# Sums of a block product chained in PSUM, the splits of a left factor spread over the next pair, and another order of the first loads of W_out

## The chip, the cores and the metric

The kernel runs on one core of a Trainium2 chip. What counts is the device time of one execution in microseconds (us). It was run three times: 2336.66, 2331.77 and 2335.1 us, median 2335.1 us. Engines are named as in the profile: PE is TensorE (its matmuls; PEld is its loading of weights), DVE is VectorE, ACT is ScalarE, POOL is GpSimd, SP is SyncE, which issues the loads. POOL issues the stores.

## The reference

One layer of an encoder trunk on x of 1024 tokens by 1024 features, float32: a half-step feed-forward network, a token mixing, and a second half-step feed-forward network, each between two norms.

```python
def _swiglu(x, w_in, w_out):                       # w_in 1024 x 5632, w_out 2816 x 1024
    g, u = jnp.split(x @ w_in, 2, axis=-1)
    return (jax.nn.silu(g) * u) @ w_out

h = _swiglu(_rms_norm(x, ffn1_pre_norm), ffn1_w_in, ffn1_w_out)
x = x + 0.5 * _rms_norm(h, ffn1_post_norm)
m = _token_mixing(_rms_norm(x, mix_pre_norm), w_mix_in, ..., w_mix_out, pos)
x = x + _rms_norm(m, mix_post_norm)
h = _swiglu(_rms_norm(x, ffn2_pre_norm), ffn2_w_in, ffn2_w_out)
x = x + 0.5 * _rms_norm(h, ffn2_post_norm)
```

`_token_mixing` projects its input once (`u @ w_in`, 6656 columns) into queries, keys, values and gates of a retention (its queries and keys get a rotary embedding) and of a neighbourhood attention, computes both, gates and projects them. The change touches the two feed-forward networks and that projection.

## The kernel before, in words

**Numbers in two parts.** A float32 product is made from three matmuls: each operand is split into a high part (a copy into the matmul format by ACT, L61) and a low part (the rest, a subtraction on DVE, L62). `mm3` (L86) multiplies high by high, high by low and low by high into one PSUM bank of 128 x 512. A product of a 128 x 512 weight block with a 512 x 512 quarter of x is four such groups, 12 matmuls.

**Seven products in place of eight.** x (transposed, 1024 x 1024) is held as the seven left operands of Winograd's form of Strassen's scheme: a11, a12, a22 and the sums s1 to s4 (class `Winograd`). A *pair* (`Pairs.run`, L364) takes two weight columns blocks, g (b11, b21) and u (b12, b22), forms four combinations t1 to t4 of them on DVE, multiplies seven times, and combines the seven banks into four results c11, c12, c21, c22. The lines of the combinations: ACT copies the bank of a11 into c11 (L377); DVE adds s2's bank to that for c12 (L382), a12's for c11 (L385), s3's bank to c12 for c21 (L390), s1's to c21 for c22 (L393) and to c12 (L394), a22's to c21 (L398), s4's to c12 (L401). `out(j)` gives the tile of result j, `done(j)` is called when it is complete. The products run in the order a11, s2, a12, s3, s1, a22, s4; each has its own bank, of six. `behind` only fixes an order on DVE. PE, DVE and ACT work through their own instructions in the order in which the scheduler has put them, and wait for each other by semaphores.

**Led pairs.** While x is still being normed and transposed, `lead` and `leads` already make the products a11 and a12 of the first pairs. The first three stay in their banks ("held"); further ones ("saved": three in FFN 1, one in FFN 2, none in the mixing projection) are copied to SBUF. These pairs have five products left when their turn comes.

**Input projection** (`ffn_in`, L405): 22 pairs, each of a gate and an up column. `done` applies silu to the gate results on ACT (L415) and multiplies by the up results on DVE (L417); the two multiplies are called up0 and up1 in the prediction, after the halves of the tile `gt` that they fill. Then `put` is called.

**Left factors of the output projection** (`LeftFactors`, L422): G = silu(g) * u becomes the left operand of the second matrix product, again in Winograd's form. Two successive pairs give a group of four blocks. When the second is there, POOL forms the four sums s1 to s4 (L441), and for each of the seven factors ACT makes a high part in a buffer `gth` (L447; four of them), DVE a low part in place (L448), and POOL stores both to DRAM (L68), 256 KB each. All seven are called one after the other at the end of the group's second pair, in the order a11, s1, s3, a22, s2, a12, s4. There are eleven groups in each network.

**Output projection** (`ffn_out`, L513): seven products of eleven steps each; step n needs one block of G (`Blocks`, L453, a load of 0.5 MB on SP) and one 128 x 512 block of W_out or of a combination of it. W_out lies in four quadrants, `tiles[i][j]`, each in three loads of 1, 1 and 0.75 MB. `LOADS` (L33) names the steps at which the twelve loads are issued: the first quadrant's at 0, 2 and 4, after the blocks of G of steps 0 and 1, 3, 5. The first four steps take their blocks of the first quadrant from loads of their own (L618). POOL forms the combinations t1 to t4 in `prepare` (L633) from steps 8, 19, 24 and 30 on. G's buffers and most tiles of W_out lie where the input projection had its operands, so their loads wait for its last matmuls. SP issues in order.

**The mixing projection** (L1163 to L1201): twelve pairs, four plain, then rotary and silu pairs in turn, and two sigmoid pairs. `done` rotates a rotary pair's results, two halves on POOL and two on DVE (`rotate`, L868 to L871), or applies the function on ACT, and stores the result. The results lie in buffers `ev`, six.

## Time and profile before

| | |
|---|---|
| runs | 2336.66, 2331.77, 2335.1 us |
| profiled execution | 2335.32 us, of which 2333.2 us are the span from the first to the last instruction |
| mean granted clock of PE | 0.989 |
| moved by DMA | 442.03 MB, mean 189 GB/s |

The stages by the trace: norm and leading products of FFN 1 up to 69 us, its input projection to 468 us, its output projection to about 700 us, the mixing to about 1673 us (the pairs of its projection from 749 to 1034 us), the leading products of FFN 2 to 1700 us, its input projection to 2104 us, its output projection to the end.

How to read the lines of the profile: a row of a timeline has the start in us from the span's start, the duration in us, engine, line of the kernel, operation, tile written <- tiles read, and, in square brackets, how long the engine was idle before and what ended that. Rows of the chain that ended last have start, duration, what. A row of a table of stretches has the stretch, its length, busy time (and instructions) of PE, PEld, DVE, ACT, POOL, then the granted clock of PE (1.00 is full), the mean busy share of the DMA engines and GB/s. In a group's row "wl<-wraw,wh" is the tile written and those read.

### The profile page before, as it was taken

Reading aid. Unit: us, or ns where it says so; the run is one execution under the profiler, and the core shown is the slowest. Engines: PE = TensorE matmul, PEld = TensorE weight load, DVE = VectorE, ACT = ScalarE, POOL = GpSimd, SP = SyncE. Lnnn points to the kernel's source line nnn. Section 1 sums busy time; section 2 is a strip of 40 time slices with the busy share of each in tenths; the row PEclk is TensorE's granted clock in tenths of the full one; section 3 lists DMA queues with packets and bytes.
Section 4 is the critical chain, followed back from the end, with each engine's and each line's share of the span. In section 5 each row is a group of like instructions: output and inputs, shape, how many; then the busy total and the mean of one; then the engine's idle time right before and its main releaser. Section 6 shows DMA issues by size and latency. Waiting matters only on the chain.

```text
span 2333.2 us, 30479 instructions
## 1 busy us (share of the span) xinstructions
PE 2230.0 (96%) x10288; PEld 1839.0 (79%) x10288; DVE 1677.9 (72%) x2833; ACT 1010.2 (43%) x2102; POOL 806.1 (35%) x889
## 2 busy tenths in 40 slices
PE   6999999989997999999999999999799999999997
PEld 5778888868886887777888888787578888887886
DVE  7888887844459768969875687546988888884443
ACT  6433443422335222248885675315544433443232
POOL 5333424259424134411001222101443333426942
PEclk9999999999999999999999999999999999999999
DMA  4445444498545442257654466766534534449764
GB/s 144 148 141 176 143 156 148 168 388 296 204 162 188 169 167 100 89 186 243 214 170 169 163 220 227 264 222 206 168 127 149 185 140 173 140 149 369 296 245 167
DMA packets 148220, 442.03 MB, mean 189 GB/s; under 512 B 18465, under 2 KB 46241, under 8 KB 145953
## 3 DMA queue, kind: packets, MB, share of 16 engines
q1 hardware_dynamic: 109344, 312.13, 39.6%
q0 software_dynamic: 38720, 127.96, 14.7%
q8 instruction: 82, 1.34, 0.2%
q14 instruction: 74, 0.60, 0.1%
HBM read 303.70 MB, written 140.51 MB: 190 GB/s over the span
## 4 chain that ended last, share of the span: by engine, by line
PE 59%; issue 13%; DVE 12%; POOL 6%; DMA 6%; ACT 3%; POOLq 0%; SPq 0%; DVEq 0%; ACTq 0%
PE ps L90 18%; PE ps L88 18%; PE ps L89 18%; DVE wl L62 3%; POOL cmb L441 2%; DMA g1s<-gth 1%; DMA g<-g0a 1%; PE pt L89 1%; PE pt L90 1%; PE pt L88 1%; DMA wraw<-in_dram 1%; ACT wh L61 1%; POOL rstd L98 1%; DVE tmp L118 1%; DVE t L379 1%
## 5 line engine op out<-in xcount | busy, mean ns | idle before, releaser
L62 DVE TENSOR_TENSOR wl<-wraw,wh 128x512 fp32r<-128x512 f32 x516 | 382.9, 761 | 80.4 <-ACT wh L61 79.2
L61 ACT CAST wh<-wraw 128x512 fp32r<-128x512 f32 x524 | 306.0, 618 | 247.7 <-DVE wraw L396 67.9
L62 DVE TENSOR_TENSOR wl<-x,wh 128x512 fp32r<-128x512 f32 x146 | 137.8, 956 | 192.1 <-ACT wh L61 191.0
L88 PE MATMUL ps<-wh,g 128*128 128x512 f32 x484 | 191.5, 397 | 11.3 <-DMA g<-g0a 6.4
L89 PE MATMUL ps<-wl,g 128*128 128x512 f32 x484 | 191.1, 395 | 0.0
L90 PE MATMUL ps<-wh,g 128*128 128x512 f32 x484 | 190.4, 393 | 0.0
L61 ACT CAST wh<-x 128x512 fp32r<-128x512 f32 x146 | 88.6, 620 | 216.4 <-PE pt L90 93.0
L441 POOL TENSOR_TENSOR cmb<-gt 128x512 f32<-128x512 f32 x44 | 63.7, 1464 | 320.6 <-DVE gt L417 320.6
L543 POOL TENSOR_TENSOR x<-x 128x512 f32<-128x512 f32 x110 | 158.8, 1469 | 34.2 <-DMA x<-in_dram 24.2
L415 ACT ACTIVATE c<-c 128x512 f32<-128x512 f32 x88 | 55.5, 631 | 147.0 <-DVE c L398 93.8
L88 PEld LDWEIGHTS ps<-wh,g 128*128 128x128 f32 x484 | 92.2, 191 | 33.4 <-ACT wh L61 7.4
L61 ACT CAST wh<-t 128x512 fp32r<-128x512 f32 x58 | 36.0, 621 | 182.9 <-DVE t L379 175.8
L90 PE MATMUL ps<-a22h,wl 128*128 128x512 f32 x280 | 110.3, 394 | 3.6 <-DVE wl L62 3.6
L90 PE MATMUL ps<-a12h,wl 128*128 128x512 f32 x280 | 109.8, 392 | 3.2 <-DVE wl L62 3.2
L88 PE MATMUL ps<-a11h,wh 128*128 128x512 f32 x280 | 111.0, 397 | 0.7 <-ACT a11h L61 0.7
L88 PE MATMUL ps<-a22h,wh 128*128 128x512 f32 x280 | 110.6, 395 | 0.1
L88 PE MATMUL ps<-a12h,wh 128*128 128x512 f32 x280 | 110.3, 394 | 0.0
L89 PE MATMUL ps<-a11l,wh 128*128 128x512 f32 x280 | 110.0, 393 | 0.0
L90 PE MATMUL ps<-a11h,wl 128*128 128x512 f32 x280 | 109.9, 392 | 0.0
L89 PE MATMUL ps<-a22l,wh 128*128 128x512 f32 x280 | 109.8, 392 | 0.0
L89 PE MATMUL ps<-a12l,wh 128*128 128x512 f32 x280 | 109.1, 390 | 0.0
L89 PEld LDWEIGHTS ps<-wl,g 128*128 128x128 f32 x484 | 92.3, 191 | 20.1 <-DVE wl L62 1.2
(373 smaller groups left out, 6490.9 us busy)
## 6 DMA issues: line engine op xcount, KB each, us to landing
wraw<-in_dram SPq DMA_DIRECT2D x221, 512.0 KB, 4.2
g<-g0s SPq DMA_DIRECT2D x44, 512.0 KB, 4.9
g<-g1s SPq DMA_DIRECT2D x44, 512.0 KB, 4.4
g<-g0a SPq DMA_DIRECT2D x33, 512.0 KB, 3.3
g<-g1a SPq DMA_DIRECT2D x33, 512.0 KB, 4.4
x<-in_dram SPq DMA_DIRECT2D x16, 1024.0 KB, 12.2
g0s<-gth POOLq DMA_DIRECT2D x44, 256.0 KB, 4.1
g0s<-cmb POOLq DMA_DIRECT2D x44, 256.0 KB, 4.5
```

Of the source, the lines that this page charges most:

```text
L61: nc.scalar.copy(h, src)
L62: (eng or nc.vector).tensor_tensor(l, src, hf, ALU.subtract)
L88: mm(ps, a[0], b[0], start=start, stop=False)
L89: mm(ps, a[0], b[1], start=False, stop=False)
L90: mm(ps, a[1], b[0], start=False, stop=stop)
L98: self.nc.gpsimd.tensor_tensor(r[:, :n], ms, self.mhalf[:, :n], ALU.pow)
L118: nc.vector.scalar_tensor_tensor(xn[:, bs], x[:, bs], r[:, 0:1], gain[:, bs], op0=ALU.mult, op1=ALU.mult)
L379: tt(t2, b22, t1, ALU.subtract)
L415: nc.scalar.activation(gate[j], gate[j], AF.Silu)
L441: eng.tensor_tensor(s[o], a, b, op)
L543: e = nc.gpsimd.tensor_tensor(out, a, b, ALU.subtract).ins
```

## The change

In `Pairs`:

- The products of a pair run in the order a11, a12, s2, s1, s3, s4, a22. s2's product goes onto the bank that holds a11's (the sum is c12's first part), s3's onto the same bank, a22's onto the same again; s4's goes onto s1's bank. `mm3` and `product` get an argument for that. Between them ACT copies the bank's present state out: c11 (a11's bank), c12 (after s2), and c22 (s1's bank). DVE adds a12's bank to c11, the chain's bank to c22 after s3, s1's bank with s4's sum to c12, and that is all: three adds from PSUM in place of seven. c21 is read from the bank itself by `done`.
- A saved pair, whose a11 is in SBUF, starts the chain with s2 in a new bank, and DVE adds a11 to each of c12, c22 and c21.
- `between` is called after every product.

In `ffn_in` and `LeftFactors`: the seven splits of a group are kept in a list, and `between` makes one of them after each product of the next pair, in the order a11, a12, a22, s1, s3, s2, s4; what is left is made when the next group comes or at the end. POOL's four sums stay where they were.

In `ffn_out`: G's block of step 0 and then the three loads of the first quadrant are issued ahead of everything else, the other nine at other steps; t4 starts at step 34 instead of 30. In FFN 2 the twelve W_out tiles are handed out in another order of addresses. In the mixing projection there are ten `ev` buffers instead of six, and `done` reads c21 from the bank.

```diff
-LOADS = (0, 2, 4, 6, 9, 12, 14, 17, 20, 23, 26, 29)
+LOADS = (6, 9, 12, 15, 18, 22, 28, 33, 38)
...
-    def mm3(self, ps, a, b, start, stop):
+    def mm3(self, ps, a, b, start, stop, onto=False):
...
-        mm(ps, a[0], b[0], start=start, stop=False)
+        mm(ps, a[0], b[0], start=start, stop=False, skip_group_check=onto)
...
+        self.between = lambda: None
...
-    def product(self, a, b, eng=None):
-        bank = self.c.bank()
+    def product(self, a, b, eng=None, bank=None):
+        onto = bank is not None
+        if not onto:
+            bank = self.c.bank()
         ah, al = self.x.op(a)
         b = self.c.piece(b, eng)
         for k in range(4):
-            self.c.mm3(bank, [p[:, k * P:(k + 1) * P] for p in b], (ah[:, k], al[:, k]), k == 0, k == 3)
+            self.c.mm3(bank, [p[:, k * P:(k + 1) * P] for p in b], (ah[:, k], al[:, k]), k == 0 and not onto, k == 3, onto)
+        self.between()
         return bank
...
-        p1 = self.begun[i][0] if i in self.begun else self.product("a11", b11)
+        begun = self.begun.get(i)
+        saved = self.held <= i < self.held + self.saved
+        p1 = begun[0] if begun else self.product("a11", b11)
         c11 = out(0)
-        for p, s in self.pieces(p1):
-            nc.scalar.copy(c11[:, s], p)
+        if not saved:
+            nc.scalar.copy(c11, p1)
         self.behind(tt(t1, b12, b11, ALU.subtract))
         tt(t2, b22, t1, ALU.subtract)
-        p6 = self.product("s2", t2)
+        p2 = begun[1] if begun else self.product("a12", b21)
+        for (p, s), (q, _) in zip(self.pieces(p2), self.pieces(p1 if saved else [c11[:, r] for _, r in self.pieces(p2)])):
+            tt(c11[:, s], p, q, ALU.add)
+        done(0, c11)
+        chain = self.product("s2", t2, bank=None if saved else p1)
         c12 = out(2)
-        tt(c12, p6, c11, ALU.add)
-        p2 = self.begun[i][1] if i in self.begun else self.product("a12", b21)
-        for p, s in self.pieces(p2):
-            tt(c11[:, s], p, c11[:, s], ALU.add)
-        done(0)
-        self.behind(tt(t3, b22, b12, ALU.subtract))
-        p7 = self.product("s3", t3)
-        c21 = out(1)
-        self.last = tt(c21, p7, c12, ALU.add).ins
+        if saved:
+            for p, s in self.pieces(p1):
+                tt(c12[:, s], chain[:, s], p, ALU.add)
+        else:
+            nc.scalar.copy(c12, chain)
         p5 = self.product("s1", t1)
         c22 = out(3)
-        tt(c22, p5, c21, ALU.add)
+        nc.scalar.copy(c22, p5)
+        self.behind(tt(t3, b22, b12, ALU.subtract))
+        self.product("s3", t3, bank=chain)
+        self.last = tt(c22, chain, c22, ALU.add).ins
+        if saved:
+            for p, s in self.pieces(p1):
+                tt(c22[:, s], c22[:, s], p, ALU.add)
+        done(3, c22)
+        self.product("s4", b22, bank=p5)
         tt(c12, p5, c12, ALU.add)
-        done(3)
+        done(2, c12)
         tt(t4, b21, t2, ALU.subtract)
-        p4 = self.product("a22", t4)
-        tt(c21, p4, c21, ALU.add)
-        done(1)
-        p3 = self.product("s4", b22)
-        tt(c12, p3, c12, ALU.add)
-        done(2)
+        self.product("a22", t4, bank=chain)
+        c21 = chain
+        if saved:
+            c21 = out(1)
+            for p, s in self.pieces(p1):
+                tt(c21[:, s], chain[:, s], p, ALU.add)
+        done(1, c21)
...
+    pairs.between = put.step
...
-                nc.scalar.activation(gate[j], gate[j], AF.Silu)
+                nc.scalar.activation(gate[j], src, AF.Silu)
...
+    put.drain()
...
+        self.drain()
         s = [self.tmp.tile([P, 4, P], F32, tag="cmb", name="cmb", bufs=4).rearrange("p k t -> p (k t)")
...
-        for n in ("a11", "s1", "s3", "a22", "s2", "a12", "s4"):
...
+        self.later = [lambda n=n, a=a: self.split(n, j, a) for n, a in
+                      zip(("a11", "a12", "a22", "s1", "s3", "s2", "s4"), (a11, a12, a22, s[0], s[2], s[1], s[3]))]
...
+    def split(self, n, j, a):
+        c = self.c
+        h, l = self.parts.tile([P, 512], F32R, tag="gth", name="gth", bufs=4), a.bitcast(F32R)
+        c.nc.scalar.copy(h, a)
+        c.nc.vector.tensor_tensor(l, a, h.bitcast(F32), ALU.subtract)
+        for q, p in enumerate((h, l)):
+            c.store(self.dst[n][j][:, q * 512:(q + 1) * 512], p.bitcast(F32))
...
+    def step(self):
+        if self.later:
+            self.later.pop(0)()
...
+    def drain(self):
+        while self.later:
+            self.step()
...
-    loads = dict(zip(LOADS, ((0, 0, 1), (0, 0, 2), (0, 0, 0),
-                             *((i, j, n) for i, j in ((0, 1), (1, 1), (1, 0)) for n in range(3)))))
+    loads = dict(zip(LOADS, ((i, j, n) for i, j in ((0, 1), (1, 1), (1, 0)) for n in range(3))))
...
-        for f, n0 in zip((t1, t2, t3, t4), (8, 19, 24, 30)):
+        for f, n0 in zip((t1, t2, t3, t4), (8, 19, 24, 34)):
...
+    operand(0)
+    for n in (1, 2, 0):
+        load(0, 0, n)
     for n, (i, k) in enumerate(steps):
...
-            return pa.tile([P, 512], F32, tag="ev", name="ev", bufs=6)
+            return pa.tile([P, 512], F32, tag="ev", name="ev", bufs=10)
...
-            def done(j):
+            def done(j, src):
                 h = j % 2
+                if j not in parts:
+                    part(j)
+                if fn not in ("rotary", None):
+                    nc.scalar.activation(parts[j], src, fn)
+                elif src is not parts[j]:
+                    nc.scalar.copy(parts[j], src)
                 if fn == "rotary":
                     rotate(turners[j], half(), parts[j], *tabs[h])
-                elif fn is not None:
-                    nc.scalar.activation(parts[j], parts[j], fn)
...
-    tiles = [[[w2.tile([P, 4, 512], F32, tag="x", name="x", bufs=12) for _ in range(3)] for _ in range(2)]
-             for _ in range(2)]
+    tiles = [w2.tile([P, 4, 512], F32, tag="x", name="x", bufs=12) for _ in range(12)]
+    tiles = [[[tiles[n] for n in m] for m in q] for q in (((3, 0, 11), (4, 5, 6)), ((2, 9, 10), (7, 8, 1)))]
```

More of the change, by code (lines that the diff above doesn't have):

```diff
@@ L84, in load_w @@
         return [self.piece(raw[:, b * 512:(b + 1) * 512]) for b in range(2)]
-    def mm3(self, ps, a, b, start, stop):
+    def mm3(self, ps, a, b, start, stop, onto=False):
         mm = self.nc.tensor.matmul
-        mm(ps, a[0], b[0], start=start, stop=False)
-        mm(ps, a[0], b[1], start=False, stop=False)
-        mm(ps, a[1], b[0], start=False, stop=stop)
+        mm(ps, a[0], b[0], start=start, stop=False, skip_group_check=onto)
+        mm(ps, a[0], b[1], start=False, stop=False, skip_group_check=onto)
+        mm(ps, a[1], b[0], start=False, stop=stop, skip_group_check=onto)
     def bank(self, tag="ps", bufs=6):
@@ L427, in __init__ @@
     def __init__(self, c, tmp, parts, dst):
-        self.c, self.tmp, self.parts, self.dst = c, tmp, parts, dst
+        self.c, self.tmp, self.parts, self.dst, self.later = c, tmp, parts, dst, []
     def __call__(self, i, gt):
@@ L441, in __call__ @@
             eng.tensor_tensor(s[o], a, b, op)
-        a = dict(zip(Winograd.NAMES, (a11, a12, a22, *s)))
-        for n in ("a11", "s1", "s3", "a22", "s2", "a12", "s4"):
-            h = self.parts.tile([P, 512], F32R, tag="gth", name="gth", bufs=4)
-            l = a[n].bitcast(F32R)
-            c.nc.scalar.copy(h, a[n])
-            c.nc.vector.tensor_tensor(l, a[n], h.bitcast(F32), ALU.subtract)
-            for q, p in enumerate((h, l)):
-                c.store(self.dst[n][j][:, q * 512:(q + 1) * 512], p.bitcast(F32))
+        self.later = [lambda n=n, a=a: self.split(n, j, a) for n, a in
[13 more added lines that the diff above has]
+            self.step()
 class Blocks:
@@ L1129, in done_nv @@
     def done_nv(t, b):
-        e = evpool[0].tile([P, 512], F32, tag="ev", name="ev", bufs=6 if len(evpool) == 1 else 4)
+        e = evpool[0].tile([P, 512], F32, tag="ev", name="ev", bufs=10 if len(evpool) == 1 else 4)
         nc.scalar.copy(e, b)
@@ L1181, in part, with done @@
                 return parts[j]
-            def done(j):
+            def done(j, src):
                 h = j % 2
+                if j not in parts:
[4 more added lines that the diff above has]
+                    nc.scalar.copy(parts[j], src)
                 if fn == "rotary":
                     rotate(turners[j], half(), parts[j], *tabs[h])
-                elif fn is not None:
-                    nc.scalar.activation(parts[j], parts[j], fn)
                 c.store((f, g)[j // 2][:, h * 512:(h + 1) * 512], parts[j])
```

## The prediction

> **What bounds the kernel now.** I read the busy table and the chain that ended last first, then a table of two long stretches, then PE's waits.

> ```profile
> PE 2230.0 (96%) x10288; PEld 1839.0 (79%) x10288; DVE 1677.9 (72%) x2833; ACT 1010.2 (43%) x2102; POOL 806.1 (35%) x889
> PE 59%; issue 13%; DVE 12%; POOL 6%; DMA 6%; ACT 3%; POOLq 0%; SPq 0%; DVEq 0%; ACTq 0%
> ```

> ```profile
> 155.00:465.00 310.00, 310.00 (x1369) 256.78 (x1369) 255.08 (x384) 125.03 (x220) 110.80 (x144) 1.00 0.45 156
> 1760.00:2090.00 330.00, 330.00 (x1456) 272.84 (x1455) 275.93 (x414) 135.94 (x240) 123.44 (x161) 1.00 0.45 157
> ```

> The columns of the second fence are the stretch, its length, the busy time of PE, PEld, DVE, ACT and POOL, the clock, the DMA share and GB/s. These are the steady parts of the two input projections: PE is busy for all of it at full clock, so TensorE sets the end there and nothing else does. 310 us over 1369 matmuls is 0.2264 us each; a product (12 matmuls) takes 2.72 us, a pair of seven products 19.0 us. DVE is busy 82% of that time and holds nobody up. The change leaves the matmuls as many as they were, so in 640 us it has nothing to win: taking adds off DVE is worth something only where PE waits for DVE or ACT, at the edges:

> ```profile
> PE ps L88 <- ACT wh L61: 12.3, 9, 2.8
> PE ps L90 <- DVE wl L62: 10.6, 13, 3.6
> PE ps L88 <- DMA g<-g0a: 6.4, 3, 2.6
> ```

> (total, times, longest.) In the steady parts it can only lose, if it gives PE a wait that wasn't there. It adds four per pair. A chained product begins by adding onto a bank, so it must come after whoever reads that bank: s2's first matmul waits for ACT's copy of c11, s3's for ACT's copy of c12, s4's for the copy of c22, and a22's for DVE's add of c22. Before, a product started in any free bank of six.

> **G's splits, one per product of the next pair.** Every second pair POOL makes four sums of a group (L441), and ACT and DVE split seven factors (L447, L448). All of it used to stand where no product needed ACT soon; now ACT's copies of a12 and a22 of the finished group stand in ACT's order directly ahead of the copy of the next pair's c11, for which s2 waits. The rows of such a group before:

> ```profile
> 1992.11 2.92 POOL L441 TENSOR_TENSOR cmb<-gt 128x512 f32<-128x512 f32 x2 [15.21 <-DVE gt L417]
> 1995.11 3.50 POOL L441 TENSOR_TENSOR cmb<-gt,cmb 128x512 f32<-128x512 f32 x2
> 1991.95 0.68 DVE L62 TENSOR_TENSOR wl<-wraw,wh 128x512 fp32r<-128x512 f32 x1
> 1995.07 0.69 DVE L448 TENSOR_TENSOR gt<-gt,gth 128x512 fp32r<-128x512 f32 x1 [2.44 <-POOL cmb L441]
> 1995.68 1.78 DVE L62 TENSOR_TENSOR wl<-wraw,wh 128x512 fp32r<-128x512 f32 x1
> 1997.47 0.58 ACT L377 COPY c<-ps 128x512 f32<-128x512 f32 x1
> g0s<-gth POOLq DMA_DIRECT2D x44, 256.0 KB, 4.1
> ```

> A DVE operation on two SBUF operands takes 0.68 us and the next can start 0.6 later; the one at 1995.68, begun inside POOL's 1995.11 to 1998.61, took 1.78. POOL's two sums took 2.92 and 3.50 us, 1.3 to 1.8 each. So the two engines hold each other up.

> Now the chain of the new order, with 0 at the first matmul of s4 of the odd pair A; a22 of A, a11 and a12 of the next pair B follow, so s2 of B is due at 4 x 2.72 = 10.9. s4 ends at 3.1; DVE's add to c12, a low part and the multiply up0 take it to 5.2. POOL's first sum needs up0: 5.2 to 6.9 (DVE's two low parts for B beside it), the second to 8.65. The second reads a11 of the group, whose low part DVE writes in place next; DVE stands at it until 8.7 and finishes at 9.4. Behind it in DVE's order is the multiply up1, ready since 6.5; like the row at 1995.68 it meets POOL's third sum and ends at 11.1. ACT then copies a12 (needs up1) and a22, 0.6 each, and only then c11 of B: 12.75. s2 starts there instead of at 10.9: a stall of 1.9 us. Bounds: with no clash of the engines the same chain ends at 10.7 to 11.0 (stall 0.1 at most); if both later sums take 1.8 and the multiply a little more, 2.5. I take 1.9, since the rows show this very sequence (a low part right after the sum that it waited for, and the next DVE operation slow). Later in B, ACT's copies of s2's and s4's factors wait for a buffer whose store must land (4.1 us at the median) ahead of c12's copy; that ends about when s3 is due, worth 0 to 1 us more. DVE, POOL and ACT have no slack to give PE back, PE being full.

> The splits run during pairs 2, 4, ... 20 of the 22. Those behind the led pairs (six in FFN 1, four in FFN 2) are 8 and 9: 17 x 1.9 = **+32 us** (0 to 45).

> **Does a stall cost clock too?**

> ```profile
> 490.60 0.77 PE L88 MATMUL ps<-wh,g 128*128 128x512 f32 x1 [2.41 <-DMA g<-g0a]
> 490.00:494.00 4.00, 3.40 (x9) 2.71 (x10) 0.00 (x0) 0.00 (x0) 0.00 (x0) 0.57 1.03 427
> 1060.87 1.09 PE L766 MATMUL pt<-ident,s 128*128 128x128 f32 x6 [2.02 <-DVE s L756]
> 1060.00:1064.00 4.00, 2.72 (x16) 2.13 (x17) 3.94 (x13) 3.22 (x9) 1.23 (x2) 1.00 0.85 261
> ```

> After an idle gap of 2.41 us the clock's mean was 0.57 over 4 us, which is 1.7 us lost; after one of 2.02 it stayed at 1.00. My stall of 1.9 lies below, so I add nothing here; that is what the range's top is about. [...] The row at 490.60 disagrees, so the sum goes by the row; I give the rule a tenth of the forecast's chance.

> **The mixing projection.** Rotary pairs alternate with silu pairs. Half of the rotations run on POOL, half on DVE, and this is what they do to each other now:

> ```profile
> 940.47 1.66 POOL L868 TENSOR_TENSOR ev<-ev,tab 64x512 f32<-64x512 f32 x1 [0.68 <-DVE ev L401]
> 945.60 1.62 POOL L871 TENSOR_TENSOR ev<-ev 128x512 f32<-128x512 f32 x1
> 940.90 1.78 DVE L62 TENSOR_TENSOR wl<-wraw,wh 128x512 fp32r<-128x512 f32 x1
> 944.29 3.47 DVE L62 TENSOR_TENSOR wl<-wraw,wh 128x512 fp32r<-128x512 f32 x2
> 942.73 0.50 PE L90 MATMUL ps<-a12h,wl 128*128 128x512 f32 x1 [0.43 <-DVE wl L62]
> 946.12 0.50 PE L90 MATMUL ps<-s3h,wl 128*128 128x512 f32 x1 [0.38 <-DVE wl L62]
> 879.87 0.50 PE L88 MATMUL ps<-s2h,wh 128*128 128x512 f32 x1 [1.19 <-ACT wh L61]
> ```

> While POOL rotates, each DVE operation takes a turn of 1.7 us, and PE waits 0.4 + 0.4 (about 1.1 with the matmuls' slow starts). In the new order the c11 copy of the silu pair stands on ACT behind the cast of s3's operand, the cast waits for DVE's t3, and t3 stands behind a last rotation on DVE while POOL rotates: the add to c12 at 5.0, one operation to 5.6, then four at 1.7 (7.3, 9.0, 10.7, 12.4), t3 13.0, cast 13.6, copy 14.2 at most, 13.8 if POOL's turns are 1.6: s2, due at 10.9, stalls about 3.0 where 1.1 was lost. That is 1.9, and as the gap is over 2.41 another 1.7 of clock: 3.6, of which I take 3.3, as the gap's length decides. Four such pairs: +13. The second rotary pair waits at 879.87 already; there the add to c11 moves ahead of t1 and s2 stalls about 3: +3. Together **+16** (-6 if the engines don't clash, to +20).

> **The led pairs.** They have five products, 13.6 us, but DVE's work of a full pair.

> ```profile
> 112.12 0.50 PE L88 MATMUL ps<-s2h,wh 128*128 128x512 f32 x1 [1.90 <-ACT wh L61]
> 139.70 0.79 PE L90 MATMUL ps<-a22h,wl 128*128 128x512 f32 x1 [3.57 <-DVE wl L62]
> 148.89 0.50 PE L88 MATMUL ps<-s2h,wh 128*128 128x512 f32 x1 [1.62 <-ACT wh L61]
> 138.00:148.00 10.00, 7.57 (x20) 5.65 (x20) 6.50 (x11) 2.20 (x4) 3.83 (x8) 0.66 0.99 350
> 1703.31 0.50 PE L90 MATMUL ps<-s2h,wl 128*128 128x512 f32 x1 [1.50 <-DVE wl L62]
> ```

> Before, DVE had 4 preparations, 5 low parts, 7 adds and 2 multiplies per pair, 18 x 0.61 = 11.0, and each second pair 7 low parts of G and four clashes of 1.1 more: 11.0 + (4.3 + 4.4) / 2 = 15.3, over 13.6. After, an unsaved led pair has 3 adds, so 12.9, under it; a saved one 6, 14.7. So PE should stop waiting there but for some 1.4 us: the three waits of FFN 1 are 7.1 us, the clock 0.34 x 10 = 3.4: **-9** (-10.5 to 0). FFN 2 has fewer: **-2**.

> **W_out's first quadrant at once.** SP now issues three loads (2.75 MB) ahead of G's block for step 1. All wait for the last matmul of the projection.

> ```profile
> 468.31 0.33 SPq L464 DMA_DIRECT2D g<-g0a  x1
> 470.11 0.56 SPq L527 DMA_DIRECT2D x<-in_dram  x1
> DMA to landing us min/median/max: 9.8/9.8/9.8
> 477.13 23.11 DMA g<-g0a
> 500.37 0.62 PE L88 MATMUL ps<-wh,g 128*128 128x512 f32 x1 [2.61 <-DMA g<-g0a]
> 2104.38 0.33 SPq L464 DMA_DIRECT2D g<-g1a  x1
> 2106.22 0.42 SPq L464 DMA_DIRECT2D g<-g1a  x1
> DMA to landing us min/median/max: 9.3/9.3/9.3
> 2107.78 0.47 PE L88 MATMUL ps<-wh,g 128*128 128x512 f32 x1 [0.75 <-DMA g<-g1a]
> 2118.98 0.80 PE L88 MATMUL ps<-wh,g 128*128 128x512 f32 x1 [2.79 <-ACT wh L61]
> ```

> In FFN 1 the five transfers from 468.31 to the one at 470.11 (its time to landing is the 9.8) brought 3.25 MB by 479.9, 11.6 us after the first issue. Step 1, due 2.5 us after it when step 0's twelve matmuls are done, will wait for as much: 9 us. But the block of step 8 landed at 477.13 + 23.11 = 500.24 behind 7.75 MB, and has the same bytes ahead of it in the new order; PE reached step 8 then, at 500.37, by several small waits, and will reach it then by one long one. So nothing is lost, and one spell of half clock fewer: -1 (-5 to +4). In FFN 2 the fifth transfer landed 11.1 us after the first issue, a wait of 8.6 at step 1 and 1.7 to 3.4 of clock, for the 0.75 and 2.79 (with slow starts and half clock some 8) that go: +2 (0 to +6). Together **+1**. The later loads stay four steps or more ahead of their use, and ten buffers for six only take waits off ACT: 0.

> **Sum.** 32 + 16 - 9 - 2 + 1 = +38 on the profiled execution, 2335.3 us (span 2333.2 and 2.1 around it; the runs' median is 2335.1): **2373 us**.

> **The rivals.**
> 1. Faster. The engines pass each other and the copies come in time: G +2, mixing -6, leads -12, starts +1, so -15: 2320. For it: DVE has four operations fewer a pair, so its place in time moves against POOL's. Against: the chain from up0 over two sums to a11's low part is one of data, whatever DVE's load. 0.13.
> 2. Shorter stalls: up1 slips in ahead of POOL's third sum, 1.1 us less: G 17 x 0.7 = 12, mixing +6, leads -11: +8, 2343. For it: one operation's luck decides; against: at 1995.11 POOL took its turn at once. 0.10.
> 3. Clock: the gap at G's splits reaches 2.4 us, and each costs 2.5 + 1.7: 17 x 4.2 = 71 for 32: 2412. For it: 0.5 us is missing, and a store's landing may add it; against: 2.02 and 1.9 kept full clock. 0.14.
> 4. Chaining does nothing that PE feels and nothing else holds: leads alone, or all cancel: 2335. 0.05.

> **How the numbers follow.** The forecast has 0.58, and its own range is 2350 to 2395. To leave out no more than 2 in 10 the range takes in the second rival and half of the third: 2340 to 2404. A change within 0.2%, 4.7 us, can't be told from none. Faster 0.14, same 0.07, slower 0.79.

> **What would show it.** Right: in the steady stretches PE is no longer busy throughout, and each second pair shows a wait of a first matmul on s2's factor for ACT's copy of c11, 1.3 to 2.5 us, behind two G copies. Near 140 us the wait of 3.57 is gone. Step 1 of each output projection waits 8 to 9 us for G, and step 8 begins some 32 us after the first issue. Wrong: PE full in the steady stretches, or gaps there that name a store's landing or a weight instead of the copy.

## The result: 2467.9 us, and the profile after

The changed kernel takes 2467.92 us (median of 4 runs, 2464.3 to 2471.45) where the kernel before takes 2333.43: 1.0578 times as long (95% interval 1.055 to 1.0605), +134 us. The forecast was +38 us and 2340 to 2404. The sign was right, and most of the loss fell in the two input projections, as forecast; the size was 3.5 times too small.

The busy table of the page and the chain that ended last, of the changed kernel:

```profile
PE 2273.5 (92%) x10288; PEld 1863.8 (75%) x10288; DVE 1542.4 (62%) x2616; ACT 1064.5 (43%) x2217; POOL 818.1 (33%) x889
PE 41%; issue 28%; DVE 11%; POOL 8%; DMA 8%; ACT 3%; POOLq 0%; SPq 0%; ACTq 0%; DVEq 0%
```

DVE has 135 us less to do, as meant. PE does the same 10288 matmuls and yet is busy 43.5 us longer: some of them ran at half clock. Its share of the chain fell from 59% to 41%. The waits of PE (total, times, longest), then the two input projections as stretches (length, PE, PEld, DVE, ACT, POOL, clock, DMA share, GB/s):

```profile
PE ps L89 <- ACT gt L399: 40.8, 20, 3.3
PE ps L89 <- ACT c L386: 30.4, 16, 2.0
PE ps L89 <- ACT ev L386: 17.5, 6, 4.3
...
PE ps L89 <- DVE gt L405: 11.5, 3, 5.2
PE ps L89 <- DMA g<-g0a: 10.7, 1, 10.7
PE ps L89 <- DMA g<-g1a: 10.6, 1, 10.6
```

```profile
168.00:517.00 349.00, 316.14 (x1326) 255.23 (x1325) 211.72 (x309) 134.90 (x245) 110.18 (x143) 0.97 0.39 136
1825.00:2234.00 409.00, 372.01 (x1551) 300.73 (x1550) 246.58 (x362) 155.94 (x282) 128.68 (x163) 0.96 0.37 131
```

In the new kernel's lines L386 is ACT's copy of c11 (c in the feed-forward networks, ev in the mixing projection), L399 its copy of c12 and L405 DVE's add to c22. The top three rows and that of L405 are waits that the chained banks brought; the two rows on DMA belong to the changed loads. PE, full in these stretches before, stands idle 33 and 37 us there, at a clock of 0.97 and 0.96.

Since both traces have the same number of matmuls, a stage can be cut in each at the same matmul number. The granted clock is either 1.00 or 0.50 in these traces; a stretch at 0.50 is called a spell of half clock. Length of each stage in us, and in brackets what it lost to half clock (half the length of its spells). The led pairs are cut within 3 us of their end; the outputs' first parts are the first 132 and 96 us of the two output projections before:

| stage | before | after | difference | forecast |
|---|---|---|---|---|
| FFN 1 led pairs | 97.0 (3.4) | 97.1 (3.4) | +0.1 | -9 |
| FFN 1 input, rest | 302.4 (0) | 351.3 (11.9) | +48.9 | } +32 |
| FFN 2 input, rest | 344.2 (0) | 401.7 (17.1) | +57.5 | } |
| mixing pairs | 284.9 (1.7) | 303.8 (11.0) | +18.9 | +16 |
| FFN 2 led pairs | 59.1 (0) | 64.3 (3.4) | +5.2 | -2 |
| outputs' first parts (1, 2) | 131.7, 95.8 (6.8) | 132.9, 102.2 (13.6) | +7.6 | +1 |
| all else | 1018.2 (13.5) | 1016.5 (13.4) | -1.7 | 0 |
| span | 2333.2 (25.4) | 2469.7 (74.0) | +136.5 | +38 |

One group of G in the steady part of FFN 2, in the timelines of the changed kernel (DVE, ACT, POOL, PE; start, duration, in brackets the idle time before and what ended it), and one piece of the chain of waits through it:

```profile
1926.29 0.69 DVE L471 TENSOR_TENSOR gt<-gt,gth 128x512 fp32r<-128x512 f32 x1 [2.42 <-POOL cmb L462]
1926.90 1.78 DVE L436 TENSOR_TENSOR gt<-c,gt 128x512 f32<-128x512 f32 x1
...
1928.71 1.14 ACT L470 CAST gth<-gt 128x512 fp32r<-128x512 f32 x2 [4.75 <-DVE gt L436]
1929.76 0.57 ACT L386 COPY c<-ps 128x512 f32<-128x512 f32 x1
...
1935.63 0.62 ACT L470 CAST gth<-cmb 128x512 fp32r<-128x512 f32 x1 [3.22 <-DMA g1a<-gth]
1937.39 0.62 ACT L470 CAST gth<-cmb 128x512 fp32r<-128x512 f32 x1 [1.13 <-DMA g1a<-gth]
1937.91 0.62 ACT L434 ACTIVATE c<-c 128x512 f32<-128x512 f32 x1
1938.44 0.56 ACT L399 COPY gt<-ps 128x512 f32<-128x512 f32 x1
...
1930.36 1.09 POOL L68 DMA_DIRECT2D g1a<-gth  x2
...
1930.38 0.50 PE L89 MATMUL ps<-s2h,wh 128*128 128x512 f32 x1 [1.96 <-ACT c L386]
1939.06 0.53 PE L89 MATMUL ps<-s3h,wh 128*128 128x512 f32 x1 [2.94 <-ACT gt L399]
```

```profile
1930.91 6.38 DMA g1a<-gth
```

The first four rows, down to the copy of c11, are the chain that the prediction drew: a11's low part waits 2.42 us for POOL's second sum, up1 behind it takes 1.78 in place of 0.68, the two copies of G come, then c11's copy, and s2 has idled 1.96 us (forecast 1.9). The forecast did not work out the rest. The copies of s2's and s4's factors need a buffer back, so they wait for the two stores issued from 1930.36 on; the second lands 6.38 us after its issue, and c12's copy stands behind it and silu. s3 idles 2.94 us.

### The profile page after: what moved, and what is told of

Its sections match the earlier page's. It is cut to its first block, busy times and chain, and to the rows that moved or that the text cites. A ratio compares the mean times of both kernels' runs of the same rounds, so it can differ in the third digit from the quotient of the medians.

```text
span 2469.7 us, 30186 instructions
## 1 busy us (share of the span) xinstructions
PE 2273.5 (92%) x10288; PEld 1863.8 (75%) x10288; DVE 1542.4 (62%) x2616; ACT 1064.5 (43%) x2217; POOL 818.1 (33%) x889
## 4 chain that ended last, share of the span: by engine, by line
PE 41%; issue 28%; DVE 11%; POOL 8%; DMA 8%; ACT 3%; POOLq 0%; SPq 0%; ACTq 0%; DVEq 0%
PE ps L89 12%; PE ps L91 12%; PE ps L90 12%; POOL cmb L462 3%; DVE wl L62 2%; DMA g1a<-gth 2%; DMA g0a<-gth 1%; DVE gt L436 1%; PE pt L90 1%; PE pt L89 1%; PE pt L91 1%; POOL rstd L99 1%; PE pt L800 1%; DVE gt L471 1%; PE ps L781 1%
## 5 line engine op out<-in xcount | busy, mean ns | idle before, releaser
L62 DVE TENSOR_TENSOR wl<-wraw,wh 128x512 fp32r<-128x512 f32 x516 | 387.4, 775 | 114.0 <-ACT wh L61 113.6
L61 ACT CAST wh<-wraw 128x512 fp32r<-128x512 f32 x524 | 307.7, 618 | 235.8 <-PE ps L90 114.7
L62 DVE TENSOR_TENSOR wl<-x,wh 128x512 fp32r<-128x512 f32 x146 | 138.8, 961 | 203.4 <-ACT wh L61 202.7
L89 PE MATMUL ps<-wh,g 128*128 128x512 f32 x484 | 190.7, 395 | 21.4 <-DMA g<-g0a 10.7
L90 PE MATMUL ps<-wl,g 128*128 128x512 f32 x484 | 190.5, 394 | 0.0
L61 ACT CAST wh<-x 128x512 fp32r<-128x512 f32 x146 | 89.4, 621 | 227.7 <-PE ps L91 104.4
L462 POOL TENSOR_TENSOR cmb<-gt 128x512 f32<-128x512 f32 x44 | 72.3, 1661 | 307.8 <-DVE gt L436 307.8
L405 DVE TENSOR_TENSOR gt<-ps,gt 128x512 f32<-128x512 f32 x44 | 30.4, 691 | 198.6 <-issue 159.1
L89 PE MATMUL ps<-s2h,wh 128*128 128x512 f32 x232 | 99.4, 428 | 51.9 <-ACT c L386 30.4
L61 ACT CAST wh<-t 128x512 fp32r<-128x512 f32 x58 | 36.1, 622 | 250.4 <-DVE t L388 248.3
L89 PE MATMUL ps<-s3h,wh 128*128 128x512 f32 x232 | 100.2, 432 | 42.3 <-ACT gt L399 40.8
L90 PE MATMUL ps<-a22l,wh 128*128 128x512 f32 x280 | 111.2, 397 | 0.0
L90 PE MATMUL ps<-a11l,wh 128*128 128x512 f32 x280 | 110.5, 395 | 0.0
## 6 DMA issues: line engine op xcount, KB each, us to landing
g0s<-gth POOLq DMA_DIRECT2D x44, 256.0 KB, 5.8
g0s<-cmb POOLq DMA_DIRECT2D x44, 256.0 KB, 5.8
```

What stands on the lines that cost most here:

```text
L61: nc.scalar.copy(h, src)
L62: (eng or nc.vector).tensor_tensor(l, src, hf, ALU.subtract)
L89: mm(ps, a[0], b[0], start=start, stop=False, skip_group_check=onto)
L90: mm(ps, a[0], b[1], start=False, stop=False, skip_group_check=onto)
L405: self.last = tt(c22, chain, c22, ALU.add).ins
L462: eng.tensor_tensor(s[o], a, b, op)
```

## The experiments

Seven kernels. Each is compared with the kernel before, which ran beside them: its median was 2333.0 us beside the first four and 2334.83 us beside the last three. Stages and waits are those of one profiled execution of each.

**Six buffers for G's high parts.** In FFN 1 the six take the place of the saved products, so from the fourth group on.

```diff
-        h, l = self.parts.tile([P, 512], F32R, tag="gth", name="gth", bufs=4), a.bitcast(F32R)
+        h, l = self.high(j), a.bitcast(F32R)
...
+        ffn_in(c, fin, fp, LeftFactors(c, early, fp, gl[0], lambda j: (
+            fp.tile([P, 512], F32R, tag="gth", name="gth", bufs=4) if j < 3 else
+            early.tile([P, 512], F32R, tag="lead", name="gth", bufs=6))))
...
+        ffn_in(c, fin, fp, LeftFactors(c, cmb, fp, gl[1], lambda j: (
+            fp.tile([P, 512], F32R, tag="gth", name="gth", bufs=6))))
```

> The changed kernel with six buffers for the high parts of G in place of four (in FFN 1 from pair 7 on, in FFN 2 throughout). Landing theory: ACT's copies of s2's and s4's factors stand ahead of the copy of c12 and wait for a store to land (5.2 and 6.4 us at 1930 us); with six buffers they wait for none, so the 17 waits of s3 (42 us) go, the 5.3 us wait of a22 near 1815 us goes, and the half clock behind them (some 24 of 32 us): 2468 - 42 - 5 - 24 = about 2397 us. The 16 waits of s2 (33 us) stay. Rival, ACT's copy of c12 is late for another reason (its order behind silu, POOL): the waits of s3 stay, within 10 us of 2468.

2414.85 us, 1.0355 (1.0335 to 1.0375). Its waits of PE:

```profile
PE ps L89 <- ACT c L386: 30.0, 16, 2.0
...
PE ps L89 <- DVE gt L405: 7.9, 3, 4.6
PE ps L89 <- ACT gt L399: 4.9, 4, 2.2
```

s3's waits fall from 40.8 us to 4.9 (the longest of the four is behind a group of FFN 1 that still has four buffers), s2's stay as they were. So the landing of the stores was what s3 waited for. a22's wait in FFN 2's led pairs falls from 5.2 us to 1.0 (the pairs from 64.3 to 56.4 us); its waits stay in FFN 1's led pairs, which have four buffers still. The time is 18 us above the expected 2397. By the trace the input projections and led pairs gave back 61 us net where 71 were expected, and the mixing pairs and the stage behind them, where nothing was changed, took 4.5 and 6.8 us more: their half clock is 14.7 us more, their idle time no more. By the last section waits of one length had half clock behind them in some places and not in others, so I count this as luck.

**The splits at once, the sums chained.**

```diff
-                      zip(("a11", "a12", "a22", "s1", "s3", "s2", "s4"), (a11, a12, a22, s[0], s[2], s[1], s[3]))]
+                      zip(("a11", "s1", "s3", "a22", "s2", "a12", "s4"), (a11, s[0], s[2], a22, s[1], a12, s[3]))]
+        self.drain()
```

> The changed kernel with all seven splits called at the end of the group's second pair, in the order of before; the sums stay chained. Chain theory: what costs is that a product must wait for ACT's copy of its bank while ACT also has G's copies to make, however they are called; the copies of c11 and c12 still stand behind some of G's, so PE is not full in the steady parts: 2420 to 2465 us. Rival, calling them one per product is the cause: the steady parts are full again, 2468 - 106 = about 2362 us.

2413.23 us, 1.0343 (1.0324 to 1.0363): below 2420, the least that was expected, but far from 2362. Its first input projection and one group there:

```profile
172.00:490.00 318.00, 304.06 (x1321) 246.52 (x1320) 213.15 (x307) 136.13 (x244) 109.05 (x142) 1.00 0.43 149
```

```profile
215.60 0.50 PE L89 MATMUL ps<-s2h,wh 128*128 128x512 f32 x1 [0.75 <-ACT c L386]
221.98 0.50 PE L89 MATMUL ps<-s3h,wh 128*128 128x512 f32 x1 [0.60 <-ACT gt L399]
```

The same two copies are waited for, only less long: 14 of 318 us are idle, none at half clock. So the waits do not need the spread splits; spreading them, in the change's other order, makes the waits longer. The chain comes with a new order of the products and with ACT's copies in place of DVE's adds; these were not tried apart.

**The splits spread, the sums not chained.** The kernel before with `LeftFactors` and the calls of `between` from the change:

```diff
             self.c.mm3(bank, [p[:, k * P:(k + 1) * P] for p in b], (ah[:, k], al[:, k]), k == 0, k == 3)
+        self.between()
         return bank
```

> The kernel before with G's splits called one after each product of the next pair, sums not chained. Chain theory: without the chain no product waits for ACT's copies, so the steady parts stay full: 2325 to 2345 us. Rival, spreading the splits is what costs: 2400 us or more.

2327.76 us over 10 runs, 0.9975 (0.9961 to 0.9988): faster than the kernel before by some 6 us.

```profile
165.00:460.00 295.00, 295.00 (x1303) 244.36 (x1302) 244.39 (x367) 119.18 (x209) 99.26 (x142) 1.00 0.45 159
```

PE is full again. The led pairs take 93.0 and 56.0 us in place of 97.0 and 59.1. So the part of the change that I charged with the loss is, by itself, a gain, and the led pairs' gain which I gave to the chain (fewer adds) comes with it and without the chain: 4.0 of 9 us in FFN 1, 3.1 for 2 in FFN 2. The two parts cost through each other: the chain with the splits at once takes 2413 us, the spread splits without the chain 2328, both together 2468.

**The loads of W_out alone**, in the kernel before; the steps of the other loads, t4's start and the order of addresses in FFN 2 come with them:

```diff
...
+    operand(0)
+    for n in (1, 2, 0):
+        load(0, 0, n)
     for n, (i, k) in enumerate(steps):
```

> The kernel before with the loads of W_out alone changed. Prediction's step: one long wait at step 1 in place of several, FFN 1 about even, FFN 2 longer; by the profile after +1 and +6: 2335 to 2345 us. Rival, the loads alone cost nothing or help, since the long wait in the changed kernel comes from the late stores of G: 2325 to 2333 us.

2338.2 us over 10 runs, 1.0018 (1.0008 to 1.0029), some 4 us slower, inside the expected range.

```profile
PE ps L88 <- DMA g<-g1a: 9.3, 1, 9.3
...
PE ps L88 <- DMA g<-g0a: 8.9, 1, 8.9
```

One wait of 9 us in each output projection. FFN 1's first part takes 130.3 us in place of 131.7 (1 more was expected), FFN 2's 99.7 in place of 95.8 (6 more were).

**One sum earlier**, added to the kernel with six buffers: a11 - a21 needs only the first pair of a group.

```diff
-        for o, a, b, op in ((0, a21, a22, ALU.add), (2, a11, a21, ALU.subtract), (1, a22, s[2], ALU.subtract),
+        for o, a, b, op in ((2, a11, a21, ALU.subtract), (0, a21, a22, ALU.add), (1, a22, s[2], ALU.subtract),
```

> The changed kernel with six buffers and with one of POOL's four sums, a11 - a21, called first; it needs only the group's first pair, so it and a11's low part on DVE move a pair ahead. ACT's order stays: the copies of a12 and a22 still stand ahead of the copy of c11. Chain of data: s2's waits come from DVE standing at a11's low part until POOL's second sum is done, with up1 behind it; they go (30 us in 16 waits to 3 at most) and with them the half clock of the two projections (13.6 us to about 2): 2415 - 27 - 12 = about 2376 us. Rival, ACT's order alone is the cause (copies of G ahead of c11's): the waits stay at 2 us each, 2415 us.

2373.71 us, 1.0164 (1.014 to 1.0188), beside 2376 expected. Its waits, and up1 of the pair ahead of the wait at 284.20 us:

```profile
PE ps L89 <- ACT c L386: 8.2, 15, 0.6
...
PE ps L89 <- ACT gt L399: 2.7, 4, 1.3
```

```profile
281.81 0.68 DVE L436 TENSOR_TENSOR gt<-c,gt 128x512 f32<-128x512 f32 x1
```

up1 takes 0.68 us and no longer stands behind a sum. s2's waits fall from 30.0 to 8.2 us, the chain of data made 22 of the 30; 3 at most were expected to stay. What stays is 0.55 us in each of 15. G's copies are still ahead of c11's on ACT, which is the rival, but DVE is late there too: the three low parts ahead of up1 take 4.08 us beside POOL's sums (at 277.81) and 1.89 us in the next pair, where POOL has none then. The two were not told apart. The half clock of both input projections is gone (13.6 us to 0). That the time came out as expected has luck in it: the led pairs of FFN 1 gave 5 us that were not in the sum.

**t3 earlier too**:

```diff
         tt(t2, b22, t1, ALU.subtract)
+        self.behind(tt(t3, b22, b12, ALU.subtract))
...
         nc.scalar.copy(c22, p5)
-        self.behind(tt(t3, b22, b12, ALU.subtract))
```

> The kernel of after_gth6_early, in which also t3 is formed right after t2 in every pair instead of after s1's product. In the mixing projection the copy of c11 then no longer waits behind a cast for which t3, held up by the rotations on DVE and POOL, is late. By the prediction's chain: four of the six waits of s2 there (3.3 us each, 13 us) go, with some 6 us of half clock; the pairs of the projection take 303.8 to 308 us now, then about 290; total about 2357 us. Rival, the silu pairs' copies are late by something else (the buffers' stores, ACT's load): the projection stays above 302 us.

2361.65 us, 1.0117 (1.0102 to 1.0133). The waits of the mixing pairs:

```profile
PE ps L89 <- ACT ev L400: 9.4, 4, 2.4
...
PE ps L89 <- ACT ev L386: 4.8, 2, 4.3
```

The four waits for c11's copy go, so the cause was the one named. Four new ones come, of 2.4 us, for the copy of c12 (L400 here) instead. The mixing pairs take 296.8 us, between the 290 expected and the rival's 302. Of the 11.9 us that they gain, 10.5 are half clock and 2.8 idle time, with 1.4 the other way; so most of it is half clock, which came behind some waits and not behind others as long (last section).

**Without the chain, with both mends.** The kernel with spread splits, six buffers and the early sum, loads as before:

> The kernel before with the splits spread over the next pair (2327.8 us so far), six buffers and the early sum; the sums not chained, loads as before. No product waits for ACT here, so the steady parts stay full; what can go is at the start of the output projections, where casts of W_out stand behind copies of G that wait for a store: 2316 to 2326 us. Rival, these waits there are the loads' own: 2327 us, no change.

2324.04 us over 5 runs, 0.9951 (0.9937 to 0.9965): faster than the kernel before and inside the expected range, but not by the expected reason. The start of the output projections hardly changed (130.5 to 129.7 us in FFN 1, the same in FFN 2). The led pairs of FFN 1 went from 93.0 to 90.5 us, but the rest of that projection from 302.4 to 305.2, since PE now waits there just behind the led pairs, 1.9 us in all:

```profile
165.00:460.00 295.00, 293.06 (x1291) 241.72 (x1290) 234.61 (x368) 119.22 (x209) 101.26 (x140) 1.00 0.46 159
```

FFN 2's led pairs went from 56.0 to 58.0 us. So the two mends gain nothing in the input projections as a whole, and the interval overlaps that of the spread splits alone (0.9961 to 0.9988): the rival, no change, is not ruled out.

## Why the prediction was wrong, step by step

- **What bounds it.** Right: in the steady parts the change could only lose, and lost 106 of the 136.5 us there by which the traces differ. These 106 us are 70 of idle time, 29 of half clock and some 7 that are left over; the first matmuls behind the waits are slow (0.50 to 0.53 us in the rows above, 0.39 without a wait).
- **s2's wait for c11's copy**, 17 of 1.9 us, 32 us: right. 16 waits, 30.4 us of idle time and about 33 with the slow starts of the matmuls; the chain of data through a11's low part was shown by the early sum.
- **s3's wait for c12's copy**, "worth 0 to 1 us more", and nothing in the sum: this is the first step that failed. 40.8 us idle in 20 waits. The clause has no sum behind it, and one would have told: the second store is issued 13.5 us after s4's first matmul (s4 began at 1917.4, the issue is the 1930.91 of the chain above; the forecast's chain, with a22's copy done at 12.2, comes close to that), lands at 17.6 by the quoted median of 4.1, and the copy of s4's factor, silu and c12's copy end at 19.3, where s3 was due at 18.2. That is 1.1 us a group already. The store took 6.4 us, not 4.1, and s3 idled 2.9. Nor is it the only one: in the changed kernel the median of the row that the forecast quoted is

```profile
g0s<-gth POOLq DMA_DIRECT2D x44, 256.0 KB, 5.8
```

  Why the stores take longer was not tried. That the landing is what s3 waits for is shown by the six buffers.
- **Clock**, "My stall of 1.9 lies below, so I add nothing here": the second step that failed. 29.0 us of half clock in the two projections, and 74.0 in place of 25.4 over the span. With six buffers, where s3's waits are nearly gone, 13.6 of the 29.0 stay: the stalls of 1.9 us cost clock by themselves. The third rival put a price on it, but made it hang on the length of one gap; the last section shows gaps of one length with half clock behind them and without.
- **The mixing projection**, +16: +18.9. The four silu pairs went as drawn, with 3.1 to 3.2 us of idle time each (forecast 3.0). In the new order t3 was at 13.0 and the copy at 13.8 to 14.2 from s4's first matmul by the forecast; in the trace s2 starts 14.2 after it, with 3.1 us idle (timelines of the changed kernel; PE, DVE, ACT, PE):

```profile
903.82 0.39 PE L89 MATMUL ps<-s4h,wh 128*128 128x512 f32 x1
...
915.14 1.64 DVE L403 TENSOR_TENSOR wraw<-wraw 128x512 f32<-128x512 f32 x1
...
917.34 0.58 ACT L386 COPY ev<-ps 128x512 f32<-128x512 f32 x1
...
917.97 0.50 PE L89 MATMUL ps<-s2h,wh 128*128 128x512 f32 x1 [3.11 <-ACT ev L386]
```

  That the total came so close has luck in it. Half clock followed the waits of two of these four pairs, where the forecast had all four, and the second rotary pair, for which it had 3 us, waited twice, with 10.2 us at half clock from 942.71 on:

```profile
942.73 0.80 PE L89 MATMUL ps<-s2h,wh 128*128 128x512 f32 x1 [3.83 <-ACT wh L61]
947.05 0.80 PE L91 MATMUL ps<-s2h,wl 128*128 128x512 f32 x1 [3.10 <-DVE wl L62]
```

- **The led pairs**, -9 and -2: measured +0.1 and +5.2, the gain did not come. The wait of 3.57 us near 140 is gone as forecast, others came. DVE has the time now, but stands: its low parts of G wait for ACT's copies, these for stores, and the add to c22, for which a22 waits, stands behind them (ACT, DVE, PE, PE):

```profile
109.55 0.62 ACT L470 CAST gth<-cmb 128x512 fp32r<-128x512 f32 x1 [5.29 <-DMA g0a<-gth]
...
110.20 0.69 DVE L471 TENSOR_TENSOR cmb<-cmb,gth 128x512 fp32r<-128x512 f32 x1 [2.12 <-ACT gth L470]
...
112.83 0.50 PE L89 MATMUL ps<-a22h,wh 128*128 128x512 f32 x1 [3.80 <-DVE gt L405]
...
146.20 0.47 PE L89 MATMUL ps<-a22h,wh 128*128 128x512 f32 x1 [2.50 <-DVE gt L405]
```

  In FFN 2's led pairs one such wait takes 5.16 us, at 1815.00, and half clock 3.4 more. I had counted operations in place of following the order. The spread splits without the chain take 4 and 3 us off these pairs.
- **The loads**, +1: +7.6, of which the loads alone make 2.5 (130.3 + 99.7 against 131.7 + 95.8). Step 1 waited 10.7 us, and step 8 of FFN 1 began 34.9 us after the first issue in place of 32. The timelines of SP and PE, and the stretch behind the wait:

```profile
518.03 1.28 SPq L559 DMA_DIRECT2D x<-in_dram  x3
...
531.41 0.77 PE L89 MATMUL ps<-wh,g 128*128 128x512 f32 x1 [10.74 <-DMA g<-g0a]
...
552.95 0.39 PE L89 MATMUL ps<-wh,g 128*128 128x512 f32 x1
```

```profile
531.00:540.00 9.00, 8.59 (x27) 6.99 (x28) 3.99 (x7) 3.25 (x6) 1.92 (x4) 0.69 1.03 420
```

  The clock of 0.69 over 9 us is the 2.8 us that the forecast's "one spell of half clock fewer" left out: the long wait brought its own. The other 5.1 us were not taken apart by a run. The waits at step 1 are longer than with the loads alone (10.7 and 10.6 us against 8.9 and 9.3), and there is 3.4 us more of half clock. The forecast overlooked that the spread splits leave the last group's stores to this place: from the projection's first matmul to the end of the wait in FFN 1, POOL's stores moved 1.01 MB here and 0.26 MB with the loads alone, while the loads moved 3.6 to 3.7 MB in both.

## What to carry to other kernels

A bank on which products are chained turned each read of it into something that the next product waits for (40.8 us in 20 waits for c12's copy here, 30.4 in 16 for c11's); before it is used on a full TensorE, list what stands ahead of every such read on the reading engine, and follow that to the end, stores and their buffers included. A store's landing is not a constant (4.1 us at the median before, 5.8 after, 6.4 in the chain shown): time it by the busiest stretch in the trace, since the changed kernel will have its own. And take a change apart: here one of its three parts is by itself a gain of 6 us, and the whole costs 134 us.

## What the runs showed of the hardware

In these traces the length of a gap did not decide whether half clock followed. In that of the changed kernel, three waits of 3.18 us for the copy of c11 end at 971.88, 1013.45 and 1056.62 us; a spell of half clock begins 0.94 us behind the second (at 1014.39), and none follows the first or the third. The kernel with six buffers has nearly the same wait at two places, of which one is followed by half clock. PE's timeline, and the stretches around the waits:

```profile
216.88 0.50 PE L89 MATMUL ps<-s2h,wh 128*128 128x512 f32 x1 [1.96 <-ACT c L386]
...
300.52 0.50 PE L89 MATMUL ps<-s2h,wh 128*128 128x512 f32 x1 [1.82 <-ACT c L386]
```

```profile
214.80:218.21 3.41, 1.45 (x7) 1.12 (x7) 3.41 (x5) 3.01 (x6) 2.94 (x4) 1.00 0.61 169
218.21:221.63 3.42, 3.42 (x10) 2.68 (x9) 3.42 (x7) 2.70 (x6) 3.20 (x6) 0.50 0.89 268
296.71:300.12 3.41, 1.99 (x9) 1.31 (x7) 3.41 (x4) 1.27 (x3) 3.22 (x3) 1.00 0.20 77
300.12:303.54 3.42, 3.02 (x13) 2.49 (x14) 3.42 (x6) 3.42 (x7) 2.95 (x6) 1.00 0.79 224
```

The first wait lies within one of these stretches, and PE was busy for 1.45 of its 3.41 us; the clock of the next is 0.50. The second is split over two, 1.99 and 3.02, both at 1.00. The two rows from which the forecast took its limit differ in the same way: before, the gap of 2.41 us left 1.30 us of work in its stretch (486.89 to 490.30, the clock of the next is 0.50), and the gap of 2.02 us was split over two (1056.90 to 1060.31 and 1060.31 to 1063.73) with 1.95 and 2.45, both and the next at 1.00.

The stretches are laid by the spells. In the traces of before and of the changed kernel a spell lasts 3.41, 6.83, 10.24 or 13.65 us, all but the last of each, which runs past the end of the span; the starts lie whole multiples of 3.413 us apart (138.72 and 490.30 before, 351.58 us, 103.0 times). Both traces, cut so from where the clock's record begins (26.1 and 27.9 us into the span), have these stretches at full clock by their busy share, and behind them:

| PE busy in the stretch | next at half clock | next at full clock |
|---|---|---|
| under 0.40 | 34 | 0 |
| 0.40 to 0.50 | 6 | 5 |
| 0.50 to 0.60 | 0 | 14 |
| 0.60 and more | 0 | 1274 |
